# Moving the head norms of an encoder block between weight units, and deferring its modulation sums

## The chip, the cores and the metric

One NeuronCore of one Trainium2 chip. The metric is device time in microseconds (us) of the whole kernel, one launch. The engines named below: PE (TensorE) does matmuls and transposes, DVE (VectorE) and POOL (GpSimd) do elementwise work, ACT (ScalarE) does activations and copies, and SP issues nearly all DMA transfers. Each engine takes its own instructions in the order in which they stand in the program.

## The reference

One block of an encoder on 512 tokens of width 2048, in float32. Everything starts from one modulation vector and one projection:

```
mod  = SiLU(c) @ w_ada + b_ada          -> sh1, sc1, g1, sh2, sc2, g2   (2048 each)
h    = RMSNorm(x) * (1 + sc1) + sh1
qa, ka, va, qb, kb, vb, ga, gb = split(h @ w_in)
qa   = rope(RMSNorm(qa per head))       8 heads of 128; ka likewise, 2 heads
ya   = softmax(qa ka^T / sqrt(128)) va  (4 query heads share one key head)
yb   = neighbourhood attention of 8 heads with a relative-position bias
x    = x + g1 * ((sigmoid(ga) * (ya @ w_oa) + sigmoid(gb) * (yb @ w_ob)) @ w_out)
h2   = RMSNorm(x) * (1 + sc2) + sh2
x    = x + g2 * SwiGLU(h2);  out = RMSNorm(x)
```

## The kernel before, in words

**Products.** Float32 accuracy comes from splitting each operand into a rounded `hi` (a copy on ACT, L118) and the rest `lo` (a subtraction, L119, on VectorE or on the engine that the caller names with `eng`). A product is then three matmuls (`mm3`, L125–128). Weights arrive in units of 512 KB: one DMA into a `raw` tile (L133), `whi` on ACT, `wlo` by the subtraction, then 24 matmuls of 512 columns. There are four `raw` buffers and four each of `whi` and `wlo`. `form1` (L157) keeps weights stationary and gives a feature-by-token result; `form2` (L175) gives token-by-feature. Both call `pump()` after every unit.

**Background.** `pump()` (L147) runs one closure from the list `later`, if there is one, and then one step of the first generator in `bg`. The generators are the modulation chunks: `ada_acc` loads a part of `w_ada` and adds its rows, each times an entry of `SiLU(c)`, into an accumulator `acc` on VectorE (L259, L261); one step is one load of 512 KB, two additions of 512 columns and a `yield`. `ada_mod` (L271) sums `acc` over partitions with small matmuls against ones into the PSUM bank Y (L279) and makes a scale and a shift of it (L267–269). `ada_gate` (L283) splits `acc` into two `ada_s` tiles, sums them with two matmuls against ones (L291, L292), copies one row to an `ada_o` tile (L294) and writes it to DRAM (L295), where a later stage reads it as a row for all partitions. `acc` has two buffers; for gates it is first cleared on GpSimd (L254) and gets the bias by DMA (L255).

**The stage around the change.** After the first part (L391–441), which builds h and at the same time runs the projections of k and v, of q's first four heads and of twelve of the sixteen A gate tiles, the gate tiles `g_acc` are written to DRAM (L442–443) and their pool is released; the pool `p_a` takes the space. Its tiles `rt` (three buffers) serve `norm_rope` (L470–487). For one block of 128 tokens this norms each head (L478), multiplies with the cosine (L479, on GpSimd) and with the sine of the exchanged pairs (L481), adds (L482), transposes on PE into the PSUM bank T (L485) and splits the result (L487) into `kT` or `q`. The scale `r` is made from sums of squares on ACT (L491–496). In program order there then come: k and q of heads 0–3, four blocks each (L499–503); the split of v (L504–507); `att_a` for heads 0–3 (L553); q's second projection with the weight split on GpSimd (L556), the last A gate group (L557, again GpSimd); the norms of the new q (L559–560); `att_a` for heads 4–7 (L561); the chunks that make the second norm's scale and shift go into `bg` (L565), and the first eight B gate tiles run with them (L566, GpSimd). `att_a` (L529) does scores into bank S, a softmax on VectorE and ACT (L519–526), transposes (L542), the split into `pt`, and the product with v into bank Y.

A scheduler then orders every engine's instructions by priorities that follow program order, so PE work from later lines is drawn into the waits of the earlier ones: the matmuls of the second q projection and of the gates lie among those of the heads. `tc.high_priority()` around the sums of `ada_mod` moves them forward.

**Later.** The rest of the B gates (L631) runs with the eight `ada_gate` generators in `bg`; these go on under the products with `w_oa` (L660) and `w_ob` (L678), whose results are gated (L673) and merged (L674). In the latter, two units of `w_out` are loaded ahead (L684) and split (L687). The loop at L739 empties what is left of `bg`.

Of the kernel before, what the change touches and what calls it, by code (L numbers as in the profile page):

```python
# [12 lines left out]
F32 = mybir.dt.float32  # L13
F32R = mybir.dt.float32r
AF = mybir.ActivationFunctionType
# [3 lines left out]
P = 128  # L19
D = 2048  # L20
T = 512
NT = T // P
KT = D // P
# [11 lines left out]
QA, KA, VA, QB, KB, VB, GA, GB = 0, 1024, 1280, 1536, 2560, 3584, 4608, 6656  # L35
# [49 lines left out]
def encoder_block(ctx: ExitStack, tc, xp, c, w_ada, b_ada, norm1_w, w_in, q_norm_w, k_norm_w, tb,  # L85
                  w_oa, w_ob, w_out, norm2_w, w_gate, w_up, w_down, final_w, rope, wmask, out):
    nc = tc.nc
    V, S, G = nc.vector, nc.scalar, nc.gpsimd
# [8 lines left out]
    io = tc.alloc_tile_pool(name="io", bufs=3, side="right")  # L97
# [7 lines left out]
    def bank(tag):  # L105
        return ps.tile([P, 512], F32, tag=tag, name=tag, bufs={"mm": 4, "S": 2, "T": 1, "Y": 1}[tag])
# [4 lines left out]
    ones = const.tile([P, P], F32, name="ones")  # L111
    V.memset(ones, 1.0)
    ones_r = const.tile([P, P], F32R, name="ones_r")
# [3 lines left out]
    def split(hi, lo, src, eng=V):  # L117
        S.activation(hi, src, AF.Copy)  # L118
        eng.tensor_sub(lo, src, hi)  # L119
# [16 lines left out]
    def wsplit(w, k0, nk, c0, ncol, eng=V):  # L136
        raw, _ = unit(w, k0, nk, c0, ncol)
        hi, lo = wtile("whi"), wtile("wlo")
        split(hi[:, :nk * ncol], lo[:, :nk * ncol], raw, eng)
        v = lambda t: t[:, :nk * ncol].rearrange("p (k n) -> p k n", k=nk)  # L140
        return v(hi), v(lo)

    bg = []

    later = []

    def pump():  # L147
        if later:
            later.pop(0)()
        if bg:  # L150
            try:
                next(bg[0])
            except StopIteration:
                bg.pop(0)
                pump()
# [19 lines left out]
    def form2(w, c0, xs, evac, r0=0, eng=V, tiles=range(NT), tags=("mm",) * NT, pre=()):  # L175

        n = len(xs)
        banks = {i: bank(tag) for i, tag in zip(tiles, tags)}
        for k0 in range(0, n, 2):
            m = min(2, n - k0)  # L180
            hi, lo = pre[k0 // 2] if k0 // 2 < len(pre) else wsplit(w, r0 + k0, m, c0, 512, eng)
            for kk in range(m):
                xh, xl = xs[k0 + kk]
                for i in tiles:
                    sl = slice(i * P, (i + 1) * P)
                    mm3(banks[i], xh[:, sl], xl[:, sl], hi[:, kk], lo[:, kk], k0 + kk == 0, k0 + kk == n - 1)
            pump()
        for i in tiles:
            evac(i, banks[i])
# [38 lines left out]
    n1, n2 = vec[:, 16:32], vec[:, 32:48]  # L228
    b_sh1, b_sc1, b_sh2, b_sc2 = (vec[:, 48 + 16 * i:64 + 16 * i] for i in range(4))
    s1 = const.tile([P, KT], F32, name="s1")  # L230
    t1 = const.tile([P, KT], F32, name="t1")
    s2 = const.tile([P, KT], F32, name="s2")
    t2 = const.tile([P, KT], F32, name="t2")
# [31 lines left out]
    def ada_done(y, k0, n, s, b_s, nw, t, b_t):  # L265
        sl = slice(k0, k0 + n)
        V.tensor_add(s[:, sl], y[:, :n], b_s[:, sl])  # L267
        V.tensor_add(t[:, sl], y[:, n:2 * n], b_t[:, sl])
        V.scalar_tensor_tensor(s[:, sl], s[:, sl], 1.0, nw[:, sl], op0=ALU.add, op1=ALU.mult)

    def ada_mod(sh, sc, k0, n, to, pool=None):  # L271

        for acc in ada_acc((sc + k0 * P, sh + k0 * P), n * P, False, pool):
            if acc is None:
                yield
        with tc.high_priority():
            y = bank("Y")
            for j in range(2 * n):
                nc.tensor.matmul(y[:, j:j + 1], acc[:, j * P:(j + 1) * P], ones[:, 0:1], start=True, stop=True)  # L279
            ada_done(y, k0, n, *to)  # L280
        yield

    def ada_gate(col, q, dst):  # L283

        for acc in ada_acc((col + q * 512,), 512, True):
            if acc is None:
                yield
        hi, lo = (io.tile([P, 512], F32R, tag="io", name="ada_s") for _ in range(2))
        split(hi, lo, acc)
        y = bank("Y")  # L290
        nc.tensor.matmul(y, ones_r, hi, start=True, stop=False)  # L291
        nc.tensor.matmul(y, ones_r, lo, start=False, stop=True)  # L292
        o = io.tile([P, 512], F32, tag="io", name="ada_o")
        V.tensor_copy(o[0:1, :], y[0:1, :])  # L294
        nc.sync.dma_start(dst[q], o[0:1, :])  # L295
        yield

    def rows(dst, src):
# [8 lines left out]
    st = lambda dt: p_q.tile([P, 512], dt, tag="st", name="st", bufs=2 * NT)  # L307
    q_acc = [st(F32) for _ in range(NT)]
    rp = p_q.tile([P, NT, 2, HD], F32, name="rp")
# [3 lines left out]
    for i in range(NT):  # L313
        acc = small.tile([P, 4], F32, tag="acc4", name="acc4")
# [31 lines left out]
    sg_a = [dram.tile([P, T], F32, name=f"sga{j}") for j in range(KT)]  # L346
    sg_b = [dram.tile([P, T], F32, name=f"sgb{j}") for j in range(KT)]
# [3 lines left out]
    hT = []  # L351
# [40 lines left out]
    r = rsqrt_mean(ssq, D, NT)  # L392
    for n, (k0, k1) in enumerate(slices):
# [5 lines left out]
        hi, lo = wsplit(w_in, k0, len(ks), KA, 512)  # L399
# [10 lines left out]
        if k1 == KT:  # L410
            kv = []
# [3 lines left out]
        for c0, accs, ends in GROUPS:  # L415
# [4 lines left out]
            for k in range(a0, k1, 2):  # L420
                m = min(2, k1 - k)
                hi, lo = wsplit(w_in, k, m, c0, 512)
                ws.update({k + e: (hi[:, e], lo[:, e]) for e in range(m)})
                step(nxt, 2)
            for i, acc in enumerate(accs):
                sl = slice(i * P, (i + 1) * P)
                b = bank(next(turn))
# [25 lines left out]
    def gates(dst, base, j0, j1, eng=V):  # L453
        for j in range(j0, j1, 2):
            form1([w_in], base + j * P, 2, hT, [[bank("mm"), bank("mm")]], keep_gate(dst[j:]), eng)
# [4 lines left out]
    nw = {}  # L460
# [9 lines left out]
    def norm_rope(src, nh, i, r, w, dst):  # L470

        n = nh * HD
        h3 = lambda a: a[:, :n].rearrange("p (h d) -> p h d", h=nh)
        bt = lambda a: a.unsqueeze(1).to_broadcast([P, nh, a.shape[1]])
        a, b, rot = (p_a.tile([P, 512], F32, tag="rt", name="rt", bufs=3) for _ in range(3))
        for h in range(nh):
            hs = slice(h * HD, (h + 1) * HD)
            V.scalar_tensor_tensor(b[:, hs], src[:, hs], r[:, h:h + 1], w, op0=ALU.mult, op1=ALU.mult)  # L478
        G.tensor_mul(h3(a), h3(b), bt(rp[:, i, 0, :]))  # L479
        for e in range(2):  # L480
            V.tensor_mul(h3(rot)[:, :, e::2], h3(b)[:, :, 1 - e::2], bt(rp[:, i, 1, e::2]))  # L481
        V.tensor_add(a[:, :n], a[:, :n], rot[:, :n])  # L482
        tp = bank("T")
        for h in range(nh):
            nc.tensor.transpose(tp[:, h * P:(h + 1) * P], a[:, h * HD:(h + 1) * HD], ident)  # L485
        hi, lo = (d.rearrange("p (h t) -> p h t", h=nh)[:, :, i * P:(i + 1) * P] for d in dst)
        split(hi, lo, h3(tp))  # L487

    kT = pair(p_a, "k", 2 * T, 1)

    def rstds(srcs, nh):  # L491
        ssq = small.tile([P, 16], F32, tag="ssq16", name="ssq16")[:, :NT * nh]
        for i, src in enumerate(srcs):
            head_ssq(src, nh, ssq[:, nh * i:nh * i + nh])
        r = rsqrt_mean(ssq, HD, NT * nh)
        return [r[:, nh * i:nh * i + nh] for i in range(NT)]

    vA = []
    for i, r in enumerate(rstds(kv, 2)):  # L499
        norm_rope(kv[i], 2, i, r, nw["k"], kT)  # L500
    q = pair(p_a, "q", 4 * T, 1)
    for i, r in enumerate(rstds(q_acc, 4)):
        norm_rope(q_acc[i], 4, i, r, nw["q"], q)
    for i in range(NT):  # L504
        v = st(F32R)
        vA.append((v[:, :256], v[:, 256:]))
        split(*vA[i], kv[i][:, 256:])

    y_d = [dram.tile([P, T], F32, name=f"y{h}") for h in range(16)]

    def keep_y(h, yb):
# [40 lines left out]

    for h in range(4):  # L553
        att_a(h, q, h, 0)
    q1 = [st(F32) for _ in range(NT)]
    form2(w_in, QA + 512, hT, lambda i, b: S.activation(q1[i], b, AF.Copy), eng=G)  # L556
    gates(sg_a, GA, 12, 16, G)  # L557
    q = pair(p_a, "q", 4 * T, 1)
    for i, r in enumerate(rstds(q1, 4)):  # L559
        norm_rope(q1[i], 4, i, r, nw["q"], q)  # L560
    for h in range(4):  # L561
        att_a(4 + h, q, h, 1)
    p_a.release()
    p_q.release()
    bg.extend(ada_mod(3 * D, 4 * D, k, 2, (s2, b_sc2, n2, t2, b_sh2)) for k in range(0, KT, 2))  # L565
    gates(sg_b, GB, 0, 8, G)  # L566

# [48 lines left out]
    for half in range(2):  # L618
        v = [pair(p_b, "v", 512, NT) for _ in range(NT)]
# [58 lines left out]
    for j in range(0, KT, 2):  # L678
        form1([w_ob], j * P, 2, yT_b, [[bank("mm"), bank("mm")]],
              gated(sg_b[j:], lambda e, g, b: merge(j + e, g, b)))  # L680
        if j >= KT - 6 and len(pre) < 2:
            raw = p_pre.tile([P, 1024], F32, name="praw", tag="praw")
            k0 = 2 * len(pre)
# [11 lines left out]
    io = tc.alloc_tile_pool(name="io2", bufs=3, side="right", reuse_waits="tile")  # L695
# [32 lines left out]
    for pr in ((0, 1), (2, 3)):  # L728
        form2(w_out, 3 * 512, mT, residual(3, gate, sq2, V, x2_d), tiles=pr, tags=("mm", "mm") if pr[0] else ("S", "S"))
        for i in pr:  # L730
            r = row_rstd(sq2[i])
# [4 lines left out]
            else:  # L736
                V.tensor_scalar(lo3, lo3, r, None, op0=ALU.mult)
                V.tensor_scalar(n3[i], hi1, r, None, op0=ALU.mult)
    while bg:  # L739
        pump()  # L740
    p_pre.release()
    p_m.release()
# [130 lines left out]
    for s in range(SU):  # L873
# [6 lines left out]
        for e in range(2):  # L880
            hi, lo = w0[e] if s == 0 else wsplit(w_gate, 4 * s + 2 * e, 2, 0, 512)
# [14 lines left out]
    for n in range(FU):  # L896
        cs = []
        for w in (w_gate, w_up):
            c, v = c_tile()
# [5 lines left out]
            dst = (v[:, 0, 0], v[:, 1, 0]), (v[:, 0, 1], v[:, 1, 1])  # L905
# [73 lines left out]
    for cc in range(4):  # L979
        hi, lo = pair(p_l, f"w{cc}", 4 * 512, 1)  # L980
        for k in range(0, 4, 2):
            raw, _ = unit(w_down, f0 + k, 2, cc * 512, 512)
# [4 lines left out]
    for i in range(NT):  # L987
        sl = slice(i * P, (i + 1) * P)
        for cc in range(4):
            b = bank(next(last))  # L990
            hi, lo = wl[cc]
# [4 lines left out]
        r = row_rstd(sq3[i])  # L996
# [38 lines left out]
```

## Time and profile before

| | us |
|---|---|
| median of three runs | 2708.28 (2704.64 to 2709.36) |
| profiled execution | 2707.57 |
| its span, first to last instruction | 2705.8 |
| busy PE | 2602.3 (96%) |
| busy VectorE | 1782.6 (66%) |
| busy ACT | 968.3 (36%) |
| busy GpSimd | 132.9 (5%) |
| mean granted clock of PE | 0.986 |

In the profile a row names the source line, the engine, the tiles written and read, the shape and the count. A row of the timeline begins with its start and duration in us; in square brackets stands the idle time of the engine before it, and what released it. A row of the waits gives the total, the number of waits and the longest. `L119` is one line for every split, so its rows are told apart by their tiles: `wlo` for weights, `ql`, `kl` and `ptl` for what comes out of transposes, `ada_s` for a gate sum, `p2l` for a `w_out` unit.

### The profile page before, as it was taken

The numbers are of one execution on the slowest core, as the hardware profiler recorded it, in microseconds if no ns is written. First come the engines' busy times: TensorE is split into PE (matmuls) and PEld (weight loads), VectorE is DVE, ScalarE is ACT, GpSimd is POOL, SyncE is SP. The second block draws the span as 40 slices with busy tenths as digits, with TensorE's granted clock in tenths as the row PEclk, the third lists the DMA queues.
The fourth block names the chain that finished last, engine by engine and source line by source line (L and its number), as shares of the span: only waits on it lengthen the run. The fifth ranks groups of instructions, "written<-read, shape, count | busy, mean of one in ns | idle before, by whom it ended". The sixth has DMA issues, their size and how long they took to land.

```text
span 2705.8 us, 38742 instructions
## 1 busy us (share of the span) xinstructions
PE 2602.3 (96%) x15385; PEld 2286.1 (84%) x15385; DVE 1782.6 (66%) x2556; ACT 968.3 (36%) x1323; POOL 132.9 (5%) x90
## 2 busy tenths in 40 slices
PE   6999898999999998999889999999999999999997
PEld 5788686878888887877789999999999988888886
DVE  7994747356656566665668888888888864343227
ACT  6233344123323233322544444444444432132122
POOL 0001331300000000000010000000000000000000
PEclk9999999999999999999989999999999999999999
DMA  9873233565554677496333433333333455243332
GB/s 307 279 248 117 75 114 105 186 189 161 173 165 150 210 257 233 148 327 212 120 112 120 137 129 124 109 128 125 125 126 125 135 190 182 94 155 125 102 109 86
DMA packets 277157, 427.17 MB, mean 158 GB/s; under 512 B 17008, under 2 KB 140256, under 8 KB 274416
## 3 DMA queue, kind: packets, MB, share of 16 engines
q1 hardware_dynamic: 276640, 423.59, 47.9%
q8 instruction: 121, 1.98, 0.3%
q10 hardware_dynamic: 336, 1.11, 0.1%
q14 instruction: 60, 0.49, 0.1%
HBM read 392.11 MB, written 32.52 MB: 157 GB/s over the span
## 4 chain that ended last, share of the span: by engine, by line
PE 70%; DMA 6%; DVE 4%; ACT 1%; issue 1%; SPq 0%; POOL 0%; DVEq 0%; ACTq 0%; POOLq 0%
PE mm L128 15%; PE mm L127 15%; PE mm L126 15%; PE S L127 5%; PE S L126 5%; PE S L128 5%; DMA raw<-in_w_ada 4%; PE Y L126 2%; PE Y L127 2%; PE Y L128 2%; DVE acc L261 1%; PE T L126 1%; PE T L128 1%; PE T L127 1%; DVE wlo L119 1%
## 5 line engine op out<-in xcount | busy, mean ns | idle before, releaser
L118 ACT ACTIVATE whi<-raw 128x1024 fp32r<-128x1024 f32 (+1 forms) x465 | 453.9, 978 | 988.7 <-PE mm L127 282.1
L119 DVE TENSOR_TENSOR wlo<-raw,whi 128x1024 fp32r<-128x1024 f32 (+1 forms) x433 | 483.1, 1118 | 376.2 <-ACT whi L118 375.6
L261 DVE SCALAR_TENSOR_TENSOR acc<-raw,cact,acc 128x512 f32<-128x512 f32 (+1 forms) x368 | 275.9, 757 | 165.7 <-DMA raw<-in_w_ada 160.5
L119 DVE TENSOR_TENSOR wlo<-ta,whi 128x1024 fp32r<-128x1024 f32 x84 | 102.7, 1223 | 71.5 <-ACT whi L118 71.4
L118 ACT ACTIVATE whi<-ta 128x1024 fp32r<-128x1024 f32 x84 | 89.4, 1065 | 132.1 <-PE mm L127 132.1
L118 ACT ACTIVATE whi<-tb 128x1024 fp32r<-128x1024 f32 x84 | 89.6, 1067 | 123.9 <-PE S L127 123.9
L128 PE MATMUL mm<-x1h,wlo 128*128 128x256 f32 x400 | 110.4, 276 | 0.0
L126 PE MATMUL mm<-x1h,whi 128*128 128x256 f32 x400 | 110.4, 276 | 0.0
L127 PE MATMUL mm<-x1l,whi 128*128 128x256 f32 x400 | 110.4, 276 | 0.0
L119 DVE TENSOR_TENSOR wlo<-tb,whi 128x1024 fp32r<-128x1024 f32 x84 | 102.5, 1221 | 6.3 <-ACT whi L118 3.1
L126 PE MATMUL mm<-x0h,whi 128*128 128x256 f32 x368 | 102.7, 280 | 3.3 <-ACT whi L118 3.3
L128 PE MATMUL mm<-x0h,wlo 128*128 128x256 f32 x368 | 103.1, 280 | 0.8 <-DVE wlo L119 0.8
L127 PE MATMUL mm<-x0l,whi 128*128 128x256 f32 x368 | 102.8, 279 | 0.0
L119 POOL TENSOR_TENSOR wlo<-raw,whi 128x1024 fp32r<-128x1024 f32 x32 | 77.7, 2431 | 407.0 <-ACT whi L118 376.0
L128 PE MATMUL Y<-x1h,wlo 128*128 128x256 f32 x336 | 92.7, 276 | 0.0
L126 PE MATMUL mm<-x3h,whi 128*128 128x256 f32 x336 | 92.7, 276 | 0.0
L127 PE MATMUL mm<-x3l,whi 128*128 128x256 f32 x336 | 92.7, 276 | 0.0
L128 PE MATMUL mm<-x3h,wlo 128*128 128x256 f32 x336 | 92.7, 276 | 0.0
L126 PE MATMUL mm<-x2h,whi 128*128 128x256 f32 x336 | 92.7, 276 | 0.0
L127 PE MATMUL mm<-x2l,whi 128*128 128x256 f32 x336 | 92.7, 276 | 0.0
L128 PE MATMUL mm<-x2h,wlo 128*128 128x256 f32 x336 | 92.7, 276 | 0.0
L126 PE MATMUL S<-x2h,whi 128*128 128x256 f32 x336 | 92.7, 276 | 0.0
(1793 smaller groups left out, 7883.6 us busy)
## 6 DMA issues: line engine op xcount, KB each, us to landing
raw<-in_w_in SPq DMA_DIRECT2D x133, 512.0 KB
raw<-in_w_ada SPq DMA_DIRECT2D x256, 256.0 KB
raw<-in_w_gate SPq DMA_DIRECT2D x88, 512.0 KB
raw<-in_w_up SPq DMA_DIRECT2D x88, 512.0 KB
raw<-in_w_down SPq DMA_DIRECT2D x88, 512.0 KB
raw<-in_w_ada SPq DMA_DIRECT2D x64, 512.0 KB
raw<-in_w_out SPq DMA_DIRECT2D x38, 512.0 KB
ffr<-ffd SPq DMA_DIRECT2D x22, 512.0 KB
```

The costliest lines, as they stand in the source:

```text
L118: S.activation(hi, src, AF.Copy)
L119: eng.tensor_sub(lo, src, hi)
L126: nc.tensor.matmul(o, lh, rh, start=start, stop=False, **kw)
L127: nc.tensor.matmul(o, lh, rl, start=False, stop=False, **kw)
L128: nc.tensor.matmul(o, ll, rh, start=False, stop=stop, **kw)
L261: V.scalar_tensor_tensor(acc, part, cact[:, k:k + 1], acc, op0=ALU.mult, op1=ALU.add)
```

## The change

Three things are done.

1. `norm_rope` for k and for q's first four heads is no longer called in place, but put into `later`, so one block is issued after each of the eight units of q's second projection, which now stands ahead of heads 0–3. The split of v moves into the evacuation of that projection. The norms of q's other four heads are issued in the same way within the units of the last A gate group.
2. Nothing of this stage is left on GpSimd: the weight splits of that projection, that gate group and the first B gates, 32 subtractions, go to VectorE, and so does the cosine product, 12 instructions.
3. The sum of an `ada_mod` chunk that is made from the B gates on is put into `due` and issued two pumps later, and that of an `ada_gate` one pump later. The row of a gate sum is copied into `acc` itself instead of a tile of its own, and written out from there.

```diff
     later = []
+    due = []
 
     def pump():
+        for d in due:
+            d[0] -= 1
+        while due and due[0][0] <= 0:
+            due.pop(0)[1]()
         if later:
             later.pop(0)()
...
-    def ada_mod(sh, sc, k0, n, to, pool=None):
+    def ada_mod(sh, sc, k0, n, to, pool=None, wait=0):
 
         for acc in ada_acc((sc + k0 * P, sh + k0 * P), n * P, False, pool):
             if acc is None:
                 yield
-        with tc.high_priority():
-            y = bank("Y")
-            for j in range(2 * n):
-                nc.tensor.matmul(y[:, j:j + 1], acc[:, j * P:(j + 1) * P], ones[:, 0:1], start=True, stop=True)
-            ada_done(y, k0, n, *to)
+
+        def finish():
+            with tc.high_priority():
+                y = bank("Y")
+                for j in range(2 * n):
+                    nc.tensor.matmul(y[:, j:j + 1], acc[:, j * P:(j + 1) * P], ones[:, 0:1], start=True, stop=True)
+                ada_done(y, k0, n, *to)
+
+        if wait:
+            due.append([wait, finish])
+        else:
+            finish()
         yield
...
         split(hi, lo, acc)
-        y = bank("Y")
-        nc.tensor.matmul(y, ones_r, hi, start=True, stop=False)
-        nc.tensor.matmul(y, ones_r, lo, start=False, stop=True)
-        o = io.tile([P, 512], F32, tag="io", name="ada_o")
-        V.tensor_copy(o[0:1, :], y[0:1, :])
-        nc.sync.dma_start(dst[q], o[0:1, :])
+
+        def finish():
+            y = bank("Y")
+            nc.tensor.matmul(y, ones_r, hi, start=True, stop=False)
+            nc.tensor.matmul(y, ones_r, lo, start=False, stop=True)
+            V.tensor_copy(acc[0:1, :], y[0:1, :])
+            nc.sync.dma_start(dst[q], acc[0:1, :])
+
+        due.append([1, finish])
         yield
...
-        G.tensor_mul(h3(a), h3(b), bt(rp[:, i, 0, :]))
+        V.tensor_mul(h3(a), h3(b), bt(rp[:, i, 0, :]))
...
-    for i, r in enumerate(rstds(kv, 2)):
-        norm_rope(kv[i], 2, i, r, nw["k"], kT)
+
+    def split_v():
+        for i in range(NT):
+            v = st(F32R)
+            vA.append((v[:, :256], v[:, 256:]))
+            split(*vA[i], kv[i][:, 256:])
+
+    rk, rq = rstds(kv, 2), rstds(q_acc, 4)
     q = pair(p_a, "q", 4 * T, 1)
-    for i, r in enumerate(rstds(q_acc, 4)):
-        norm_rope(q_acc[i], 4, i, r, nw["q"], q)
-    for i in range(NT):
-        v = st(F32R)
-        vA.append((v[:, :256], v[:, 256:]))
-        split(*vA[i], kv[i][:, 256:])
-
+    later.extend(partial(norm_rope, kv[i], 2, i, rk[i], nw["k"], kT) for i in range(NT))
+    later.extend(partial(norm_rope, q_acc[i], 4, i, rq[i], nw["q"], q) for i in range(NT))
+    q1 = []
+
+    def keep_q1(i, b):
+        if i == 0:
+            split_v()
+        q1.append(st(F32))
+        S.activation(q1[i], b, AF.Copy)
+
+    form2(w_in, QA + 512, hT, keep_q1)
+    assert not later
...
     for h in range(4):
         att_a(h, q, h, 0)
-    q1 = [st(F32) for _ in range(NT)]
-    form2(w_in, QA + 512, hT, lambda i, b: S.activation(q1[i], b, AF.Copy), eng=G)
-    gates(sg_a, GA, 12, 16, G)
     q = pair(p_a, "q", 4 * T, 1)
-    for i, r in enumerate(rstds(q1, 4)):
-        norm_rope(q1[i], 4, i, r, nw["q"], q)
+    later.extend(partial(norm_rope, q1[i], 4, i, r, nw["q"], q) for i, r in enumerate(rstds(q1, 4)))
+    gates(sg_a, GA, 12, 16)
+    assert not later
     for h in range(4):
         att_a(4 + h, q, h, 1)
     p_a.release()
     p_q.release()
-    bg.extend(ada_mod(3 * D, 4 * D, k, 2, (s2, b_sc2, n2, t2, b_sh2)) for k in range(0, KT, 2))
-    gates(sg_b, GB, 0, 8, G)
+    bg.extend(ada_mod(3 * D, 4 * D, k, 2, (s2, b_sc2, n2, t2, b_sh2), wait=2) for k in range(0, KT, 2))
+    gates(sg_b, GB, 0, 8)
...
-    while bg:
+    while bg or due:
         pump()
```

## The prediction

> **What bounds the kernel now.** I read the page first, then the PE waits of the whole span, then tables by stretch, then single rows. In the page's parts 1 and 5:
> ```profile
> PE 2602.3 (96%) x15385; PEld 2286.1 (84%) x15385; DVE 1782.6 (66%) x2556; ACT 968.3 (36%) x1323; POOL 132.9 (5%) x90
> L119 POOL TENSOR_TENSOR wlo<-raw,whi 128x1024 fp32r<-128x1024 f32 x32 | 77.7, 2431 | 407.0 <-ACT whi L118 376.0
> ```
> PE is the bound: the change leaves its matmuls as they are, so only PE's idle time and its clock can move. The second line is the GpSimd work that goes to VectorE. The waits of PE (total us, times, longest), of which these belong to the work that the change touches:
> ```profile
> PE T L485 <- DVE rt L482: 9.5, 5, 3.3
> PE Y L292 <- DVE ada_s L119: 8.7, 1, 8.7
> PE S L128 <- DVE ql L119: 5.8, 2, 4.9
> PE Y L279 <- DVE acc L261: 5.2, 4, 2.2
> PE T L542 <- DVE ptl L119: 3.5, 2, 2.8
> PE mm L126 <- DVE go L449: 3.0, 1, 3.0
> PE T L485 <- DVE rs L525: 1.3, 1, 1.3
> ```
> That is 37.0 us, the most there is to win in idle time. Where they lie: the first two rows below are the same view cut to 255–315 and 480–600 us, the third to 745–765 us:
> ```profile
> PE T L485 <- DVE rt L482: 7.8, 4, 3.3
> PE Y L279 <- DVE acc L261: 3.0, 2, 2.2
> PE Y L279 <- DVE acc L261: 1.9, 1, 1.9
> ```
> The stretches (width, busy PE, PEld, DVE, ACT, POOL, then PE's granted clock, DMA share, GB/s):
> ```profile
> 272.00:330.00 58.00, 48.49 (x229) 36.96 (x227) 47.26 (x102) 21.59 (x41) 20.95 (x13) 0.94 0.23 77
> 405.00:435.00 30.00, 22.53 (x95) 16.93 (x94) 21.68 (x43) 8.28 (x14) 9.10 (x5) 0.89 0.42 128
> 435.00:480.00 45.00, 41.48 (x248) 33.13 (x246) 32.39 (x75) 22.70 (x48) 6.00 (x3) 1.00 0.29 93
> 480.00:600.00 120.00, 114.03 (x513) 93.83 (x512) 48.46 (x65) 23.60 (x25) 27.57 (x15) 1.00 0.60 191
> 745.00:765.00 20.00, 18.08 (x70) 14.71 (x69) 8.49 (x13) 5.23 (x7) 0.00 (x0) 0.83 0.44 140
> 1055.00:1080.00 25.00, 16.27 (x64) 12.98 (x63) 16.33 (x21) 8.67 (x11) 0.52 (x1) 0.80 0.62 203
> ```
> A clock below 1.00 is a second price of a gap: (1 - clock) x width is 3.5, 3.3, 0, 0, 3.4 and 5.0 us of lost matmul time, at most, since some of it falls into the idle time itself.
>
> **The change part by part.** All line numbers are those before the change.
>
> **A, k's and q's norms (L470–487) between the units of the second q projection.** Now they run in one block:
> ```profile
> 278.68 0.61 DVE L478 SCALAR_TENSOR_TENSOR rt<-st,rr,nwk 128x128 f32<-128x128 f32 x2 [5.34 <-DMA sga<-g_acc]
> 279.33 1.02 DVE L481 TENSOR_TENSOR rt<-rt,rp 128x128 f32<-128x128 f32 x2
> 280.46 0.43 DVE L482 TENSOR_TENSOR rt<-rt 128x256 f32<-128x256 f32 x1
> 283.18 2.72 DVE L478 SCALAR_TENSOR_TENSOR rt<-st,rr,nwk 128x128 f32<-128x128 f32 x2
> 293.04 2.56 DVE L119 TENSOR_TENSOR st<-st 128x256 fp32r<-128x256 f32 x1
> 295.53 0.68 DVE L482 TENSOR_TENSOR rt<-rt 128x512 f32<-128x512 f32 x1
> 283.06 2.42 POOL L119 TENSOR_TENSOR wlo<-raw,whi 128x1024 fp32r<-128x1024 f32 x1 [0.84 <-ACT whi L118]
> 292.70 2.62 POOL L119 TENSOR_TENSOR wlo<-raw,whi 128x1024 fp32r<-128x1024 f32 x1 [0.20 <-ACT whi L118]
> 280.94 0.44 PE L485 MATMUL T<-ident,rt 128*128 128x128 f32 x2 [3.34 <-DVE rt L482]
> ```
> The first row waits for the copy-out of g_acc, whose space the rt tiles take; that wait stays. The same pair of L478 takes 0.61 us, but 2.72 us when it starts while GpSimd holds a subtraction (283.06 to 285.48): a GpSimd subtraction costs VectorE up to 2.1 us there, more than the 1.22 us that it will cost on VectorE (row of p2l under E, same shape). So taking GpSimd away is, in this stage, no loss for VectorE.
>
> The Trainium skill's page "SBUF — State Buffer", section "Who interferes with whom", says that a VectorE instruction with two SBUF inputs and a GpSimd one that reads SBUF block each other for whole instructions; the trace agrees (2.72 against 0.61 us), and no term of the sum needs it.
>
> Before: 7.8 + 1.3 us idle and 3.5 us of clock, 12.6. After: the built order has 25 matmuls ahead of the first transpose, not 22; at 0.23 us (rows 1060.91 and 1061.14 under E) PE arrives 0.7 us later, at 280.94 - 3.34 + 0.7 = 278.3. VectorE is done at 278.68 + 0.61 + 0.43 (L479's product; as L482) + 1.02 + 0.43 = 281.2: 2.9 us idle stay, and half the clock loss, 1.7. Later ones come once per unit of 24 matmuls, 5.5 us, and need on VectorE for q 1.13 (L478; four at the 0.61/2 of the first row give 1.22) + 0.68 (product) + 0.75 (L481; two at 1.02/2 give 1.02 as the upper bound) + 0.68 + 0.68 (ql) + 1.22 (wlo): 5.1 to 5.5. It fits, barely. The norms issue no DMA; on ACT the splits of kh and qh (under the 5.5 us of a unit, one each) go with them, and the split of v waits for the end of the projection, ahead of head 0's last product only. What is given up: the second projection's matmuls filled the stalls of heads 0–3, and now the gate group's alone are left there, 8 units of 5.5 us for four heads. Heads 4–7 were filled by gates alone before (row 435–480: one wait of 2.8, PE 41.48 of 45), so the price is between 0 and 2.8; I take 0, since every head still has two units. Gain 12.6 - 4.6 = 8.0; from 5 (one such gap of 3.0 more) to 9.7 (no clock loss).
>
> **L479 to VectorE.** Where it ran:
> ```profile
> L479 POOL TENSOR_TENSOR rt<-rt,rp x12: 736/1285/1540, 279.4 to 424.8; 128x512 f32<-128x512 f32 x8, 128x256 f32<-128x256 f32 x4
> ```
> Eight at 0.68 and four at 0.43 add 7.2 us to VectorE, on the chain that the transposes wait for only in the first k norm (counted in A); there GpSimd's product ran beside L481, so 0.43 replaces nothing and costs 0.4.
>
> **B, the other q norms in the last A gate group.** Now:
> ```profile
> 411.91 1.54 DVE L261 SCALAR_TENSOR_TENSOR acc<-raw,cact,acc 128x512 f32<-128x512 f32 x2 [3.83 <-DMA raw<-in_w_ada]
> 415.23 0.68 DVE L119 TENSOR_TENSOR ql<-T,qh 128x512 fp32r<-128x512 f32 x1
> 427.13 2.65 DVE L482 TENSOR_TENSOR rt<-rt 128x512 f32<-128x512 f32 x1
> ```
> VectorE takes its queue in order; it stood 3.83 us at a modulation product that waited for its weights, and ql behind it held PE for 4.9 us. 427.13 is another instruction stretched (2.65 against 0.68), PE behind it 1.7. Before: 5.8 + 1.7 + 3.3 = 10.8. After, the norms are done long before heads 4–7 need them, but the order still has modulation products ahead of one ptl and ahead of head 4's first row maximum. Their price is between nothing and two waits of 3.83; the nearest row (ptl, 2.8, under C) says less than one each: I take 3.0, and 1.6 of clock. Gain 6.2, from 2 to 9.5.
>
> **C, heads 4–7 and the first eight B gates.** 3.5 (ptl) + 3.0 (go) + 3.0 (Y). One row:
> ```profile
> 469.92 0.48 DVE L259 TENSOR_SCALAR acc<-raw,cact 128x512 f32<-128x512 f32 x1 [4.36 <-DMA raw<-in_w_ada]
> ```
> This product held ptl; in the new order it stands behind the last ptl: 2.8 of the 3.5 goes. The deferral moves one sum's Y matmuls 13 matmuls later (3.0 us, so its 2.2 goes) and the next 10 earlier (2.3 us more wait): nothing, net. The go copy still follows a product. To VectorE come 9 subtractions at 1.22, 11 us, where 48.46 of 120 is busy: hidden, unless they queue behind a product (rival 2). With some of go's wait I take 4.0; from -3 (one new wait like go's) to 9.5.
>
> **D, the later sums.** At 745–765 the Y matmuls and all products keep their places; 1.9 idle and 3.4 of clock stay: 0.
>
> **E, the gate sums (L283–296).**
> ```profile
> 1065.97 1.22 DVE L119 TENSOR_TENSOR p2l<-praw,p2h 128x1024 fp32r<-128x1024 f32 x1 [2.63 <-ACT p2h L118]
> 1069.52 0.68 DVE L119 TENSOR_TENSOR ada_s<-acc,ada_s 128x512 fp32r<-128x512 f32 x1
> 1071.32 1.22 DVE L119 TENSOR_TENSOR wlo<-raw,whi 128x1024 fp32r<-128x1024 f32 x1
> 1060.91 0.39 PE L128 MATMUL mm<-y11h,wlo 128*128 128x512 f32 x1
> 1061.14 0.39 PE L291 MATMUL Y<-ada_s,ones_r 128*128 128x512 f32 x1
> 1070.25 0.79 PE L292 MATMUL Y<-ada_s,ones_r 128*128 128x512 f32 x1 [8.72 <-DVE ada_s L119]
> 1063.37 0.37 SPq L246 DMA_DIRECT2D raw<-in_w_ada  x1
> 1070.86 0.25 SPq L255 DMA_DIRECT2D acc<-in_b_ada  x1
> ```
> VectorE stood at p2l, so ada_s was late, and PE stood at Y with the next weights ready. Seven of the eight pairs of Y matmuls move 24 matmuls, 5.5 us, later. PE would start waiting at 1061.53 + 5.5 = 1067.0, ada_s is there at 1070.2: 3.2 idle, then 0.6 for the wlo that ends at 1072.5. Clock before: I take 2.0 of the 5.0, as most of it lies in the gap, and the same after. Gain 10.7 - 5.8 = 4.9; from 2 to 10.7. SP: an accumulator now stays taken until its row is copied out, so the next bias load waits for a landing and holds SP. The rows show SP standing 7.1 us at that load already, with no wait of PE for weights beside it in 1055–1080: 0, and 5.5 (one unit) if the cover were gone.
>
> **Sum.** 8.0 + 6.2 + 4.0 + 4.9 = 23.1. The profiled execution took 2707.57 us (span 2705.8); it gives 2684.5. It lies 0.7 under the median of the three runs, 2708.28: 2685.
>
> **The rivals.** **1, the waits move:** what holds VectorE is weights that land late, and these transfers stay; so A keeps 5, B 2, C 0, E 2: 2699. For it: 5.34, 3.83, 4.36 us of DMA wait in the rows. Against: GpSimd's stretched rows (2.72, 2.56, 2.65) are no DMA wait. **2, slower:** in the B gates wlo stands on VectorE behind products that wait; if each product's load is issued only when its unit begins, wait 3.83 + products 1.54 + wlo 1.22 = 6.6 us against 5.5 of PE, 1.1 over 16 units, and each form's go copies behind it 3.0 more, eight times: 41.6 lost, against 19.1 won in A, B and E, C's 4.0 lost: 2730 at worst, 2718 if half the copies are hidden. It decides once VectorE lags by more than the three weight units that four buffers hold ready, 16.5 us. Against: 48.46 of 120 busy. **3, gaps without a clock loss:** the gaps left start no slow stretch: 1.7 + 1.6 + 2.0 less lost, about 2680. For it: 435–480 and 480–600 have gaps of 2.8 and 3.0 at clock 1.00; against: 745–765 has one of 1.9 and 0.83.
>
> The Trainium skill's page "TensorE: Matmul & The Clock Gate", Part 1, has the clock drop after an idle window of about 3.4 us. By that rule rival 3 holds; the row at 745–765 speaks against it here.
>
> **4, no change:** new waits in the packed q units (5.5 against 5.5) eat the gain: 2708.
>
> **How the numbers follow.** Forecast 0.50, rival 1 0.20, rival 2 0.08, rival 3 0.15, no change 0.07. The sum's own ends are 2707.57 less 6 and less 39.4: 2702 and 2668. Range 2669 to 2703, which leaves out rival 2 and no change. About 0.2% (5 us) is what a measurement can tell from no change: faster 0.84, same 0.07, slower 0.09.
>
> **What would show it.** A: PE's wait for rt a single one of about 2.9 near 279, no L478 row over 1.2. B, C: no wait of PE for ql; ptl and max waits under 3; wait for wlo none. D: a wait of about 1.9 for acc and a clock drop. E: the wait for ada_s near 3 instead of 8.7. Wrong if PE waits for wlo in the B gates, or if transposes wait at every q unit.

## The result

The changed kernel takes 2668.64 us (median of 4 runs, 2666.26 to 2669.93) where the kernel before takes 2708.82 us (4 runs, 2704.64 to 2713.43): a ratio of 0.985, 95% interval 0.9833 to 0.9868, 40.2 us less. The forecast was 2685, with 2669 to 2703 as its range: the right direction, but 23 of the 40 us, and the measured median lies 0.4 us below the range.

The profiled execution took 2669.27 us with a span of 2667.4. Busy time by engine, from the page of the changed kernel:

```profile
PE 2593.4 (97%) x15385; PEld 2282.7 (86%) x15385; DVE 1797.7 (67%) x2600; ACT 967.0 (36%) x1323; POOL 40.6 (2%) x46
```

And PE's waits that answer to the ones shown before (total us, times, longest). The changed kernel's L266, L286 and L307 are L261, L279 and L292 before; L494 to L501 are L478 to L485; L550 and L698 are L523 and L673.

```profile
PE Y L286 <- DVE acc L266: 4.9, 4, 2.4
PE S L126 <- ACT e L550: 1.8, 1, 1.8
PE T L501 <- DVE rt L498: 1.5, 1, 1.5
PE mm L126 <- DVE o L698: 1.4, 1, 1.4
PE Y L307 <- DVE ada_s L119: 1.2, 1, 1.2
```

The reader is to see what is missing: no wait for `ql`, for `ptl` or for `go`, and the 9.5 us for `rt` are one wait of 1.5. Of the 37.0 us of waits shown before, 7.6 are left (4.9 + 1.5 + 1.2), and two new ones of 1.8 and 1.4 stand beside them.

Where the time went is read from four places that both programs pass: the first scores of the first B head, the first `w_ob` matmul, the first `w_out` matmul of the second half, and the end. The changed kernel's timeline at the first three:

```profile
617.18 0.51 PE L126 MATMUL S<-qkh 128*128 128x256 f32 x2
1018.32 0.39 PE L126 MATMUL mm<-y8h,whi 128*128 128x512 f32 x1
1124.19 0.73 PE L126 MATMUL mm<-whi,m4h 128*128 128x512 f32 x2 [3.67 <-ACT whi L118]
```

And the kernel before:

```profile
641.42 0.51 PE L126 MATMUL S<-qkh 128*128 128x256 f32 x2
1044.82 0.39 PE L126 MATMUL mm<-y8h,whi 128*128 128x512 f32 x1
1158.48 0.73 PE L126 MATMUL mm<-whi,m4h 128*128 128x512 f32 x2 [3.88 <-ACT whi L118]
1245.80 0.50 PE L126 MATMUL mm<-whi,m0h 128*128 128x512 f32 x1 [2.74 <-DVE ro L717]
```

So 24.2 us are won by the first place, 26.5 by the second, 34.3 by the third and 38.4 over the span. Of the 4.1 us behind the third, the wait of the last row, 2.74, is gone. The forecast had 18.2 (A, B and C) for the first stretch, nothing for the second, 4.9 for the third, nothing for the fourth.

In about one execution in five, of the kernel before as of the others, the matmuls of the SwiGLU stage start 4% further apart (117.8 instead of 113.3 ns in a profile of one) and the run is some 30 us longer; these are inside the medians and make the intervals of the experiments wide, so times ahead of that stage are read from the profiles too.

### The profile page after: what moved, and what is told of

It is laid out like the page before. It is cut to its first block, busy times and chain, and to the rows that moved or that the text cites. A ratio compares the mean times of both kernels' runs of the same rounds, so it can differ in the third digit from the quotient of the medians.

```text
span 2667.4 us, 38705 instructions
## 1 busy us (share of the span) xinstructions
PE 2593.4 (97%) x15385; PEld 2282.7 (86%) x15385; DVE 1797.7 (67%) x2600; ACT 967.0 (36%) x1323; POOL 40.6 (2%) x46
## 4 chain that ended last, share of the span: by engine, by line
PE 87%; DMA 5%; DVE 5%; ACT 1%; issue 1%; SPq 0%; DVEq 0%; ACTq 0%
PE mm L128 17%; PE mm L127 17%; PE mm L126 17%; PE S L126 6%; PE S L127 6%; PE S L128 6%; DMA raw<-in_w_ada 4%; PE Y L126 3%; PE Y L127 3%; PE Y L128 3%; DVE acc L266 2%; PE T L128 1%; PE T L127 1%; PE T L126 1%; DVE wlo L119 1%
## 5 line engine op out<-in xcount | busy, mean ns | idle before, releaser
L119 DVE TENSOR_TENSOR wlo<-raw,whi 128x1024 fp32r<-128x1024 f32 (+1 forms) x465 | 522.4, 1126 | 402.0 <-ACT whi L118 401.5
L266 DVE SCALAR_TENSOR_TENSOR acc<-raw,cact,acc 128x512 f32<-128x512 f32 (+1 forms) x368 | 270.1, 741 | 124.8 <-DMA raw<-in_w_ada 119.4
L127 PE MATMUL S<-x2l,whi 128*128 128x256 f32 x336 | 92.7, 276 | 0.0
```

What stands on the lines that cost most here:

```text
L127: nc.tensor.matmul(o, lh, rl, start=False, stop=False, **kw)
L266: V.scalar_tensor_tensor(acc, part, cact[:, k:k + 1], acc, op0=ALU.mult, op1=ALU.add)
```

## The experiments

Three theories stood against each other for the first stretch. The stalls theory is that of the prediction: each wait has its own cause, and where the norms stand and which engine subtracts both count. The port theory: GpSimd's reads hold VectorE, and that was nearly the whole loss. The position theory: only the new place of the norms counts.

### The engine alone, the norms alone, both, the sums alone

Only the engine:

```diff
-        G.tensor_mul(h3(a), h3(b), bt(rp[:, i, 0, :]))
+        V.tensor_mul(h3(a), h3(b), bt(rp[:, i, 0, :]))
...
-    form2(w_in, QA + 512, hT, lambda i, b: S.activation(q1[i], b, AF.Copy), eng=G)
-    gates(sg_a, GA, 12, 16, G)
+    form2(w_in, QA + 512, hT, lambda i, b: S.activation(q1[i], b, AF.Copy))
+    gates(sg_a, GA, 12, 16)
...
-    gates(sg_b, GB, 0, 8, G)
+    gates(sg_b, GB, 0, 8)
```

> Only the second part of the change: the 32 weight subtractions and the 12 cosine products on VectorE, the norms and the sums where they were. Stalls theory (each wait of PE has its own cause, and position and engine both count): the stretched VectorE rows (2.5 us and more under a GpSimd subtraction) are gone, the waits for ql behind a modulation product and for the first rt stay: 2695 to 2703. Port theory (GpSimd holding VectorE was nearly the whole loss of this stage): 2684 to 2690. Position theory (only where the norms stand matters): 2706 to 2712, as more work on VectorE in the packed block eats what it saves.

Only the norms: the changed kernel with the lines that name GpSimd (`G`) back and the sums undeferred (the gate sum's row goes through a tile of its own again, which isn't shown).

```diff
-        V.tensor_mul(h3(a), h3(b), bt(rp[:, i, 0, :]))
+        G.tensor_mul(h3(a), h3(b), bt(rp[:, i, 0, :]))
...
-    form2(w_in, QA + 512, hT, keep_q1)
+    form2(w_in, QA + 512, hT, keep_q1, eng=G)
...
-    gates(sg_a, GA, 12, 16)
+    gates(sg_a, GA, 12, 16, G)
...
-        due.append([1, finish])
+        finish()
...
-    bg.extend(ada_mod(3 * D, 4 * D, k, 2, (s2, b_sc2, n2, t2, b_sh2), wait=2) for k in range(0, KT, 2))
-    gates(sg_b, GB, 0, 8)
+    bg.extend(ada_mod(3 * D, 4 * D, k, 2, (s2, b_sc2, n2, t2, b_sh2)) for k in range(0, KT, 2))
+    gates(sg_b, GB, 0, 8, G)
```

> Only the first part: the norms between the weight units, but the subtractions and cosine products still on GpSimd and the sums undeferred. Stalls theory: the block's waits of 9 us go, since a stretched row now has a unit's 5.5 us to hide in; 2686 to 2694. Port theory: most of the loss stays, 2700 to 2706. Position theory: 2683 to 2687.

Norms and engine: the same without the lines that name G.

> The first and second part, no deferred sum. If the parts are independent, 24 us of the 40 saved come from here: 2683 to 2687, with PE's wait of about 9 us at the gate sum in the w_ob stage and the one of 2.7 us at a w_out evacuation back. If the deferral only counted because the first stage had run ahead, the gate sum's wait would be shorter here already: 2677 to 2681.

Only the sums: the kernel before with `due`, `wait=2` and the deferred gate sum.

> Only the third part, the deferred sums. Independent parts: 7.8 (gate sum in the w_ob stage) + 3.1 (w_out stage) + up to 2.2 (between the B heads): 2695 to 2699. If VectorE had to be ahead from the first stage for the gate sum to be in time: wait there of about 3 with its clock loss, 2700 to 2704.

Measured, beside one median of 2712.85 us (28 runs) for the kernel before. Ratios here are of means, not of medians; the last two columns are from one profile each, where the kernel before has 641.42 and 1044.82:

| | median us | ratio, 95% interval | first B scores, us | first `w_ob` matmul, us |
|---|---|---|---|---|
| engine only | 2677.00 (6 runs) | 0.9885, 0.9846 to 0.9924 | 613.30 | 1014.79 |
| norms only | 2706.18 (12) | 0.9969, 0.9954 to 0.9984 | 636.68 | 1036.97 |
| norms and engine | 2684.09 (11) | 0.9907, 0.9870 to 0.9943 | 613.10 | 1017.21 |
| sums only | 2701.12 (12) | 0.9970, 0.9945 to 0.9995 | 642.00 | 1041.14 |

The engine alone does all that was won in the first stretch, and more than any theory had for it: 28.1 us by the first B scores. The norms alone win 4.7 there, and on top of the engine nothing. Stalls and position theory are both refuted. Nor was it that GpSimd took longer over a subtraction (2.43 us against 1.22) and PE stood for it: PE's waits of the kernel before name GpSimd nowhere. PE's waits of the engine-only kernel:

```profile
PE Y L292 <- DVE ada_s L119: 9.3, 2, 9.0
PE Y L279 <- DVE acc L261: 2.6, 3, 1.5
PE mm L126 <- DVE ro L717: 2.4, 1, 2.4
PE T L485 <- DVE rt L482: 1.6, 1, 1.6
```

The norms still stand in one block there, and the block costs PE one wait of 1.6 us instead of 9.5 in five. With the norms spread but the subtractions still on GpSimd, a VectorE row, its GpSimd row and two of PE's waits:

```profile
303.24 2.72 DVE L499 TENSOR_TENSOR rt<-rt 128x512 f32<-128x512 f32 x1
303.03 2.38 POOL L119 TENSOR_TENSOR wlo<-raw,whi 128x1024 fp32r<-128x1024 f32 x1 [3.58 <-ACT whi L118]
```

```profile
PE T L502 <- DVE rt L499: 5.4, 3, 2.1
PE S L126 <- ACT e L551: 4.3, 1, 4.3
```

The addition that takes 0.68 us undisturbed starts 0.2 us behind the start of a GpSimd subtraction and ends 0.55 us behind its end. The units' 5.5 us do not hide that.

The sums alone change nothing in the first stretch (642.00): up to 927 us, shortly before the first gate sum, its trace has the instructions of the kernel before in the same order on every engine. The 3.7 us by which it is ahead there, and still at the first `w_ob` matmul, are therefore chance (the kernel before has its slow stretch of the clock at 753 us). Behind that the sums win. Their gate sum:

```profile
PE Y L307 <- DVE ada_s L119: 2.7, 1, 2.7
PE mm L126 <- DVE ro L733: 1.1, 1, 1.1
```

8.7 became 2.7 without any help from the first stage, so the deferral works by itself, though the median, 2701.12, lies in the range that I had set for a wait of about 3 us with its clock loss; and the wait for `ro` in the `w_out` stage, which the prediction took as untouched, falls from 2.7 to 1.1. With the norms and the engine but undeferred sums these two are back at 9.4 and 2.6.

### Is it the port, and is it the reads?

The engine switch also lets the scheduler put instructions in another order, which could itself be the gain. So the engine-only kernel was given GpSimd work that nobody waits for, in the 16 units of q's second projection and the last A gate group (`eng` names G there and no longer in the B gates; `junk` is a tile of its own; the loop in the line below runs once). On PE, VectorE, ACT and SP its order stays instruction by instruction that of the engine-only kernel.

```diff
-        split(hi[:, :nk * ncol], lo[:, :nk * ncol], raw, eng)
+        split(hi[:, :nk * ncol], lo[:, :nk * ncol], raw), eng is G and [G.tensor_sub(junk, hi[:, i:i + 1024], hi[:, i:i + 1024]) for i in range(0, 1024, 1024)]
```

> The engine switch of e1, with one more GpSimd instruction after each of the 16 weight splits of q's second projection and the last A gate group: a subtraction of 128x1024 of whi from itself into a tile that nothing reads. All other engines have e1's order. Port theory: 16 times up to 2.1 us of VectorE are held, rows of 2.5 us and more come back, and PE's waits for rt and ql with them: ratio to before 0.991 to 0.997 instead of e1's 0.9885. Order theory (e1 won because the scheduler, told of other durations, put PE's and VectorE's instructions in another order): as e1, 0.987 to 0.990.

The second writes only, but for two columns that pace it:

```diff
-        split(hi[:, :nk * ncol], lo[:, :nk * ncol], raw, eng)
+        split(hi[:, :nk * ncol], lo[:, :nk * ncol], raw), eng is G and (G.tensor_copy(junk[:, :2], hi[:, :2]), [G.memset(junk, 0.0) for _ in range(2)])
```

> The same, but GpSimd writes the unread tile (two memsets of 128x1024, paced by a copy of two columns of whi) instead of reading one: about as long on GpSimd, without its reads. If VectorE is held by GpSimd's reads only: as e1, 0.987 to 0.990, no stretched row. If any GpSimd instruction holds it: as the idle subtraction.

The idle subtraction took 2690.54 us (6 runs), the idle memset 2680.30 (6 runs), beside 2713.50 before; the ratios, 0.9896 (0.9848 to 0.9944) and 0.9894 (0.9836 to 0.9953), are too wide to tell them apart, and the idle subtraction's lies in the range that I had given to the order theory. The runs one by one and the first stretch do tell: the five shorter of the idle subtraction's runs took 2685.59 to 2692.19 us, the four shorter of the memset's 2675.05 to 2680.47, and the first B scores start at 624.84 us against 613.87. As the order is the same, order is not what sets these two apart. Timeline of the idle subtraction, VectorE, GpSimd and PE:

```profile
281.12 2.11 DVE L482 TENSOR_TENSOR rt<-rt 128x256 f32<-128x256 f32 x1
281.06 1.89 POOL L139 TENSOR_TENSOR junk_g<-whi 128x1024 f32<-128x1024 f32 x1 [2.84 <-ACT whi L118]
283.28 0.44 PE L485 MATMUL T<-ident,rt 128*128 128x128 f32 x2 [3.29 <-DVE rt L482]
624.84 0.53 PE L126 MATMUL S<-qkh 128*128 128x256 f32 x2
```

And of the idle memset, same place:

```profile
281.52 0.43 DVE L482 TENSOR_TENSOR rt<-rt 128x256 f32<-128x256 f32 x1
281.86 0.61 DVE L478 SCALAR_TENSOR_TENSOR rt<-st,rr,nwk 128x128 f32<-128x128 f32 x2
281.59 1.97 POOL L139 MEMSET junk_g<- 128x1024 f32 x2
613.87 0.53 PE L126 MATMUL S<-qkh 128*128 128x256 f32 x2
```

The same addition takes 2.11 us beside the reading instruction and 0.43 beside the writing one; the pair of L478, which starts when the memsets have run for 0.27 us, takes its usual 0.61. PE's wait of 3.29 us for `rt`, as long as the one of 3.34 before, is back with the reads alone. Sixteen GpSimd instructions whose result nobody uses cost PE 11.5 us. The Trainium skill's page "SBUF — State Buffer", section "Who interferes with whom", says this: two SBUF inputs on VectorE contend with a GpSimd instruction that reads SBUF, not with one that only writes it. Both halves agree with these rows.

### Which GpSimd work

Of the switch, only the cosine product (one line of the first diff), and only the subtractions (the other three):

> Of the engine switch only the 12 cosine products, the weight subtractions stay on GpSimd. Port theory: the weight subtractions of 2.4 us are what holds VectorE, so little changes: 0.997 to 1.000.

> Of the engine switch only the 32 weight subtractions; the 12 cosine products of 0.7 to 1.5 us stay on GpSimd. Port theory: nearly all of e1's gain, 0.988 to 0.991.

The cosine alone: 2710.07 (12 runs), ratio 0.9996 (0.9954 to 1.0039), first B scores at 636.85. The subtractions alone: 2686.22 (12), 0.9903 (0.9862 to 0.9943), 616.38. So the subtractions carry it: 25.0 of the 28.1 us.

The time for which VectorE was held can be summed: of every VectorE instruction from 255 us to the first B scores that took more than 0.2 us over 1.3 times the median of its kind (operation, tiles and shape) in the engine-only kernel, what it took over that median.

| | held VectorE, us (instructions) | first B scores later than engine only, us |
|---|---|---|
| before | 28.4 (22) | 28.1 |
| norms only | 37.0 (25) | 23.4 |
| cosine on VectorE only | 22.1 (14) | 23.5 |
| idle subtraction | 15.2 (12) | 11.5 |
| subtractions on VectorE only | 5.6 (8) | 3.1 |
| idle memset | 2.2 (3) | 0.6 |
| engine only | 1.3 (2) | 0 |

PE's loss follows the held time, for the kernel before nearly one to one; the spread norms hide a good part of it, some 13 us. That is a correlation over kernels whose orders differ; only the two idle kernels hold the order still. What stays open is how much of the rest of the 28.1 us, beyond the 11.5 that reads alone brought back with half of the subtractions, is the other order and not the port. Idle work in the B gates' units too was not tried.

### What of the change is needed

Four kernels on one chip, beside 2711.58 us (11 runs) before. The changed kernel again:

> The changed kernel itself, beside the next three on one chip: 0.983 to 0.987 of the kernel before; the first B head's scores at 617 us.

Without the two-pump delay of the second norm's sums:

```diff
-    bg.extend(ada_mod(3 * D, 4 * D, k, 2, (s2, b_sc2, n2, t2, b_sh2), wait=2) for k in range(0, KT, 2))
+    bg.extend(ada_mod(3 * D, 4 * D, k, 2, (s2, b_sc2, n2, t2, b_sh2)) for k in range(0, KT, 2))
```

> The changed kernel with the sums of the second norm's chunks back in place (no two-pump delay); the gate sums stay deferred. If that delay costs what the norms-and-engine run suggests: the first B head's scores at 613 instead of 617 us, total 3 to 5 us under the changed kernel. If it is only chance of that run: the same as the changed kernel, within 2.

Without the moved norms: the sums-only kernel with the engine-only diff.

> The changed kernel without the moved norms: k's and q's norms in one block as before. If the move brings nothing once GpSimd is out of the way: within 2 us of the changed kernel. If it does bring something: 4 to 9 us over it, with the waits of 9 us for rt partly back.

With neither: that kernel with the diff of the delay.

> Only the engine switch and the deferred gate sums: neither the moved norms nor the two-pump delay. If both are worth nothing here, this is the shortest change that keeps all of the gain: 2 to 5 us under the changed kernel; if the norms' move is worth something, over it.

| | median us (6 runs each) | ratio, 95% interval | first B scores | first `w_ob` matmul |
|---|---|---|---|---|
| changed, again | 2673.57 | 0.9849, 0.9779 to 0.9919 | 616.22 | 1015.75 |
| without the delay | 2675.39 | 0.9825, 0.9763 to 0.9888 | 616.95 | 1016.63 |
| engine and all sums | 2667.21 | 0.9801, 0.9745 to 0.9858 | 612.75 | 1012.25 |
| engine and gate sums | 2666.34 | 0.9813, 0.9749 to 0.9878 | 612.26 | 1012.71 |

The shortest change, the engine switch and the deferred gate sums, is at least as fast as the whole one; its median is 7.2 us lower, though the intervals overlap.

The two-pump delay of the other sums does nothing. With it and without it, the traces have the same instructions in the same order on every engine, from the first to the last, both with the norms moved and with the norms unmoved. (A likely reason, not tested, is that `tc.high_priority()` puts these sums in the same place either way.) So the four rows are two programs, each run twelve times, and the differences within a pair, 1.8 and 0.9 us, are noise.

The moved norms win nothing on top of the engine and rather cost something. Twelve runs of each program, on one chip, have medians of 2675.39 us with them and 2667.21 without; on another chip norms and engine took 2684.09 and the engine alone 2677.00. At the first B scores the profiles overlap: one order gave 613.10, 616.22, 616.95 and 617.18, so a single profile is good to about 4 us there, and without the moved norms it was 612.26 to 613.30. At the first `w_ob` matmul they don't: 1015.75 to 1018.32 in the four with the moved norms, 1012.25 to 1014.79 in the three without. A part of this is seen: near 405 us, among heads 0–3, PE waits for the softmax's `e` on ACT, 1.8 us in the changed kernel and 0.9 to 1.9 in the other three, and none of the three kernels with the norms unmoved has that wait. The rest stays open.

My expectation for the run without the delay, 613 us at the first B scores, was built on the norms-and-engine profile (613.10), which is the low one of those four.

Of the waits named so far the shortest version keeps these:

```profile
PE Y L307 <- DVE ada_s L119: 2.9, 1, 2.9
PE Y L286 <- DVE acc L266: 2.6, 3, 1.3
PE T L501 <- DVE rt L498: 1.3, 1, 1.3
```

## Why the prediction was wrong, point by point

**The failing step: "So taking GpSimd away is, in this stage, no loss for VectorE", and the 0.4 us of cost put on L479.** The row of 2.72 us was read as it should be, and then entered the sum at nothing. The stretched rows were left as single cases, and the gains of A and B booked to the norms' new place. The experiments turn this round: the engine alone wins 28.1 us in this stretch, the place alone 4.7, and on top of the engine nothing. With the order held still, GpSimd's reads alone, in half of the units, cost PE 11.5 us. The held time could have been summed over the stage from the trace of before, where it is 24.2 us with that trace's own medians (28.4 with those of the engine-only kernel); three stretched rows were quoted instead.

In size the miss has four parts: of the 15.3 us between the forecast gain of 23.1 and the 38.4 in the profiles, 6.0 lie in the first stretch, where this step failed, 2.3 in D, 2.9 in E and 4.1 behind it, where nothing was forecast. That the first stretch came out only 6.0 off is partly luck: most of its 18.2 had been forecast for the norms' new place, which alone is worth 4.7.

**A.** One wait for `rt` near 279 was forecast at 2.9 us; it is 1.5, at 280.94 (2.3 to 2.4 in the three other profiles with the norms moved and nothing on GpSimd). The start is the same wait for the copy-out of `g_acc`:

```profile
278.95 0.61 DVE L494 SCALAR_TENSOR_TENSOR rt<-st,rr,nwk 128x128 f32<-128x128 f32 x2 [3.04 <-DMA sga<-g_acc]
279.60 0.42 DVE L495 TENSOR_TENSOR rt<-rt,rp 128x256 f32<-128x256 f32 x1
279.94 0.49 DVE L497 TENSOR_TENSOR rt<-rt,rp 128x128 f32<-128x128 f32 x2
280.46 0.43 DVE L498 TENSOR_TENSOR rt<-rt 128x256 f32<-128x256 f32 x1
280.94 0.44 PE L501 MATMUL T<-ident,rt 128*128 128x128 f32 x2 [1.50 <-DVE rt L498]
```

The product cost 0.42, as taken. But the pair L481 was priced at 1.02 from a row that was itself stretched; free of GpSimd it takes 0.49. VectorE was done 0.3 us earlier than forecast although it started 0.3 later, and PE came later than 278.3, at 279.4. The "barely" of "it fits" came from the same row. The price of what A gives up, the filling of heads 0–3, was taken as 0: the wait for `e` near 405 us, 0.9 to 1.9, is there.

**B and C.** Forecast gains 6.2 and 4.0, kept small because the modulation products still wait for their weights. They do, but no `ql`, `ptl` or `go` wait is left, with the engine alone too: that they stood behind a waiting product was true of one moment of a VectorE that ran late. With A they came to 24.2 instead of 18.2. C also had the deferral move one sum's Y matmuls 13 matmuls later and the next 10 earlier. The deferral moves none: in the engine-only kernel, without any, these sums stand 14 later and 10 earlier, so it is the engine switch that made the scheduler move them.

**D.** Forecast 0; 2.3 us were won between the first B scores and `w_ob`. That is chance. The wait itself did not shrink in this profile (1.9 before; 0.7 and 1.0 in two other profiles of the changed kernel's order):

```profile
729.75 1.02 PE L286 MATMUL Y<-ones,acc 128*128 128x1 f32 x8 [2.41 <-DVE acc L266]
```

```profile
745.00:765.00 20.00, 20.00 (x90) 16.53 (x90) 12.00 (x14) 4.19 (x6) 3.22 (x3) 1.00 0.63 191
```

It is longer, but no slow stretch of the clock followed; 3.4 us of clock had been assumed to stay. The row of the table by stretch shows 1.00 where 0.83 stood. Of all fourteen profiles only the one before and the cosine-only one have slow steps there. The sums-only kernel, which keeps the old order up to 927 us, has none and needs 399.1 us from the first B scores to `w_ob`, where the kernel before needed 403.4 and the changed one 401.1.

**E.** Forecast 4.9; measured 7.8 (34.3 less 26.5). The mechanism was right: the Y matmuls come one unit later (six of the eight pairs by 24 matmuls, one by 12, one not at all; seven by 24 had been said), and PE waits for `ada_s` 1.2 us where 3.2 was forecast (2.1 in the changed kernel's second profile, 2.6 and 2.9 without the moved norms). With 1.2 no slow stretch came either, where the kernel before had one of 10.2 us; of the five other profiles with deferred gate sums, with waits of 2.1 to 2.9, four have a single slow step of 3.4 us, and they win 6.2 to 6.7 us in this stretch. So some 1 us of the 7.8 is luck. VectorE's queue was further ahead:

```profile
1037.37 1.23 DVE L119 TENSOR_TENSOR p2l<-praw,p2h 128x1024 fp32r<-128x1024 f32 x1 [2.66 <-ACT p2h L118]
1040.91 0.69 DVE L119 TENSOR_TENSOR ada_s<-acc,ada_s 128x512 fp32r<-128x512 f32 x1
1041.65 0.50 PE L307 MATMUL Y<-ada_s,ones_r 128*128 128x512 f32 x1 [1.18 <-DVE ada_s L119]
```

Against the first `w_ob` matmul `ada_s` starts 2.1 us earlier than before (1040.91 - 1018.32 = 22.6; 1069.52 - 1044.82 = 24.7).

**What was not looked at.** The wait of 2.74 us for `ro` in the `w_out` stage falls to 1.3 or less in every kernel with deferred gate sums and stays at 2.4 to 2.9 in all the others. The gate sums run on into that stage; the list of waits was cut off at the stages that the diff names.

**The rivals.** Rival 1 (the waits move) and rival 2 (`wlo` late on VectorE) are refuted: there is no wait of PE for `wlo` in the B gates, and the engine switch is the gain. Rival 3, gaps without a clock loss, was nearest, at 2680. Its condition held in D and E of this profile, by where the gaps fell, which the last section shows; it did not hold near 405 and 552 us, where the changed kernel has slow stretches of 3.4 and 6.8 us. With the sum's own high end, 2668, one came within a microsecond; it stood there as the sum of best cases, not as one cause.

## What to carry to other kernels

Where one VectorE row of an operation takes several times another of the same shape, look for a GpSimd instruction that reads SBUF over the same time, sum the excess over the whole stage, and put that sum into the forecast: here 28.4 us held stood beside 28.1 us of PE's time, and 15.2 us of idle work's holding beside 11.5. Durations for a new order are to be taken from rows that no such instruction touched. Then test the parts alone, and compare the built orders first: of three, one did all of the work in its stage, one rather cost something, and of the third a half did its own elsewhere and a half changed no instruction's place.

## What the runs showed of the hardware

**When the clock drops.** In all fourteen profiles PE's slow stretches begin and end on a fixed grid of 3.41 us. Taking each such step that ran at full clock, up to PE's last matmul, with the time in it in which PE was idle by the trace, the step after it was slow:

| idle time in a step of 3.41 us | steps | next one slow |
|---|---|---|
| 2.0 and more | 102 | 102 |
| 1.8 to 2.0 | 22 | 16 |
| 1.2 to 1.8 | 79 | 14 |
| under 1.2 | 10341 | 2 |

So what counts is not a gap's length but how much of it falls into one step. The gap of 2.41 us at 729.75 lies over two steps (1.9 and 0.5) and cost no clock. The one of 1.92 at 752.96 before lay in one and cost two slow steps; at 1.9 us in a step it can go either way, as the second row shows. The Trainium skill's page "TensorE: Matmul & The Clock Gate", Part 1, has a free-running window of about that length, and the drop after an idle window; here 2.0 us, some 60% of a window, is always enough, and a window need not be idle throughout.

**GpSimd waits as well.** In the memset kernel a GpSimd copy of two columns took 0.20 us at 281.33 and 1.17 at 270.18, when VectorE had begun a subtraction 0.1 us earlier and ended it at 271.31: the hold goes both ways.

```profile
270.08 1.23 DVE L119 TENSOR_TENSOR wlo<-raw,whi 128x1024 fp32r<-128x1024 f32 x1 [0.18 <-ACT whi L118]
270.18 1.17 POOL L139 COPY junk_g<-whi 128x2 f32<-128x2 f32 x1 [1.32 <-ACT whi L118]
281.33 0.20 POOL L139 COPY junk_g<-whi 128x2 f32<-128x2 f32 x1 [2.51 <-ACT whi L118]
```
